# Output projection of a hybrid encoder block as seven products of halves, with its weight sums made by adding DMAs, the convolution's norm moved into the attention loop, and normalised rows transposed once

## The chip, the cores and the metric

The kernel runs on one core of one Trainium2 chip. The metric is device time in microseconds (us) of one execution, as the median over several runs; lower is better. A core has five engines with in-order queues that meet only through semaphores: TensorE (PE, matrix multiplies and transposes, writes to PSUM), VectorE (DVE), ScalarE (ACT), GpSimd (POOL) and SyncE (SP, which here only issues DMAs). PSUM holds accumulators, SBUF everything else.

## What is computed

```python
h = rms_norm(x, norm1_g); z = h @ w_in
a, gate, q, k, v = split(z)
conv = silu(layer_norm(depthwise_conv(a * sigmoid(gate), 31 taps) + bias))     # 512 channels
attn = neighbourhood_attention(rms_norm(q), rms_norm(k), v, rpb)               # 8 heads of 64
x = x + concat(conv, attn) @ w_out                                             # 1024 x 1024 x 1024
h = rms_norm(x, norm2_g)
x = x + (silu(h @ w_gate) * (h @ w_up)) @ w_down                               # 2816 hidden
```

There are 1024 tokens (16 grid rows of 64) and 1024 channels, all in float32. Accuracy is kept by splitting each matmul operand into a high part `hi`, which a cast rounds to float32r, and a low part `lo`, which is the source less `hi`: `mac` (L110) issues three matmuls for each product of two 128-deep blocks (hi by hi, hi by lo, lo by hi). `split` (L103) makes the pair: a cast on ACT (L104), then a subtraction on DVE or POOL (L108).

## The kernel before

The order of the work is written out by hand: no scheduler moves anything. A list `woven` holds small pieces of side work; after each three matmuls PE's program pops one piece (`weave`, L119), so that the side work is issued between matmuls in a fixed place. Tiles come from rings: `G` (22 buffers of 128x1024), `R` (3 raw weight chunks), `H` (6 of 128x4096), and in PSUM `mm` (4 banks), `tp` (2 banks) and `cv` (two banks as one). A new tile waits until the one that held its buffer has been read for the last time.

**Stages, in order.** (1) The input projection for keys, convolution, queries and values, with the convolution's 31 taps beside it on DVE (L319) and, for some taps, on ACT and POOL (L344, L345). Each `step` (L411) closes one 128x512 block. (2) The attention loop (L789 to L814): 32 iterations `i`, each of them one pair of heads for one tile of 128 queries. An iteration issues the score matmuls of `i` (L615), the POOL scaling of the softmax of `i-1` (L637), the transposes of `i-2` (L646) with their evacuations on ACT and DVE (L651), bias, minimum and exponential of `i` (L628 on DVE, L630 on ACT), and the value matmuls of `i-3` (L662). The evacuations of a finished tile (`evac_hi`, `evac_lo`) and two weight chunks of `w_out`, cut in four parts each (`take_parts`, L156), go between them. (3) The output projection: eight token tiles, two halves of 512 output columns, eight 128-deep blocks, three matmuls each (`proj`, L720): 384 matmuls of 128x512 into banks `pj` (first half) and `pk` (second half). Between them, the convolution is transposed to rows (`conv_T`, L728), normalised (`conv_stats`, `conv_scale`), transposed back (L761), given its activation and split (`conv_silu`). `resid` (L775) adds each half to `x`, `norm2` and `norm2_out` (L867) make the second norm. (4) The gate and up projections as seven products of halves (Winograd's form of Strassen's scheme) for each of 22 pairs of column blocks: `products` lists them, `product` (L1013) issues 12 matmuls, `evac` (L1024) combines the seven results. The left operands `A11`, `A12`, `S1` to `S4` and `A22` are the normalised rows, their halves and sums of halves, each transposed on its own by PE (`t2_one`, L994, and `s_T`, L963) and then split. The weight sums come from `t_sums` (L893, DVE), the weight splits from `prep`. (5) The down projection, again as seven products, with sums kept in DRAM.

The weights of `w_out` come as eight chunks of 128x1024 (`want`, `issue`, `take`), in order, three in flight, each load issued by SP when the buffer of an earlier chunk comes free.

Of the kernel before, what the change touches and what calls it, by code (L numbers as in the profile page):

```python
# [7 lines left out]
F32R = mybir.dt.float32r  # L8
AF = mybir.ActivationFunctionType
# [21 lines left out]
def layout(v):  # L31
# [4 lines left out]
    gu = np.stack([f["w_gate"], f["w_up"]]).reshape(2, KB, P, FB, P).transpose(3, 0, 2, 1, 4)  # L36
    wd = f["w_down"].reshape(FB, P, D)
# [14 lines left out]
        "wo": f["w_out"],  # L52
# [15 lines left out]
def build(ctx, tc, a):  # L68
# [24 lines left out]

    def mm(name):
        return ps.tile([P, 512], F32, tag="mm", bufs=4, name=name)
# [35 lines left out]
    def want(src, name, dst, sub=(pool,)):  # L131
        chunks.append((src, name, dst, sub))

    def issue():
        if pos[0] < len(chunks):
            src, name, _, _ = chunks[pos[0]]
# [4 lines left out]
            nc.sync.dma_start(d, src)  # L141
            pos[0] += 1

    def take(n=1, ahead=True):
        for _ in range(n):
            i = pos[1]
            while pos[0] <= i:
                issue()
            _, _, dst, sub = chunks[i]
# [37 lines left out]
    wo, woq = {}, {}  # L187

    def wo_dst(d, k0):
        def dst():  # L190
            if (d, k0 // 4) not in woq:
                woq[d, k0 // 4] = H(f"wo{d}{k0}", F32R)
            q = woq[d, k0 // 4]
            o = k0 % 4 * 1024
            hl = (q[:, o:o + 1024], q[:, o + 1024:o + 2048])
            for j in range(2):
                wo[d, k0 + j] = [w[:, j * 512:(j + 1) * 512] for w in hl]
            return hl
        return dst

    for d in range(2):
        for k0 in (4, 6, 0, 2):
            want(a["wo"][k0 * P:(k0 + 2) * P, d * 512:(d + 1) * 512].rearrange("(k p) m -> p k m", p=P),
                 f"wo{d}{k0}", wo_dst(d, k0), (pool,) * 4 if d == 0 and k0 < 4 else (pool,))
# [204 lines left out]
    pend = []  # L409

    def step(post=None, n_taps=4):  # L411
        todo = pend[:]
# [251 lines left out]

    def evac_hi(s_):
        rh, cb = order[s_]
        if rh == 0:
            at[cb] = [G(f"at{cb}{w}", F32R).rearrange("p (c t q) -> p c t q", c=4, t=2) for w in range(2)]
        act.copy(at[cb][0][:, :, rh], os_[s_])

    def evac_lo(s_, cs=slice(0, 4)):
        rh, cb = order[s_]
        hi, lo = [w[:, cs, rh] for w in at[cb]]
        dve.tensor_tensor(lo, os_[s_][:, cs], hi.bitcast(F32), OP.subtract)
# [38 lines left out]
    cm, x2, xn = [], {}, {}  # L713

    def lhs(k, t):
        if k < 4:
            return [w[:, k, t * P:(t + 1) * P] for w in cm]
        return [w[:, k - 4, t // 4, :] for w in at[t % 4]]

    def proj(t, d, acc, ks):  # L720
        for k in ks:
            mac(acc, lhs(k, t), wo[d, k], k == 4, k == 3)
            weave()

    def conv_T(t):
        y = cv(f"y{t}")[:, :512] if t in (0, 3) else tp(f"y{t}")
# [4 lines left out]
    cs = {}  # L731

    def conv_stats(t, y):
        st6, mv, sd = SM(f"bs{t}", 6), SM(f"bm{t}", 2), SM(f"bd{t}", 1)
        dve.bn_stats(st6, y)
        dve.bn_aggr(mv, st6)
        act.activation(sd, mv[:, 1:2], AF.Sqrt, bias=eps)
        cs[t] = y, mv, sd
        if 1 <= t <= 4:
            conv_scale(t - 1)  # L740
        if t >= 4:
            conv_scale(t)

    def conv_scale(t):
        y, mv, sd = cs.pop(t)
        r = SM(f"br{t}", 1)
        dve.reciprocal(r, sd)
        if t % 2 == 0:
            xx = G(f"xh{t}")
            xh.extend([xx[:, :512], xx[:, 512:]])  # L750
        if t >= 6:
            dve.tensor_scalar(xh[t], y, mv[:, 0:1], r, op0=OP.subtract, op1=OP.mult)
        else:
            nb = SM(f"bb{t}", 1)
            dve.scalar_tensor_tensor(nb, mv[:, 0:1], -1.0, r, OP.mult, OP.mult)
            act.activation(xh[t], y, AF.Identity, bias=nb, scale=r)

    def conv_silu(h, c):
        y = tp(f"z{h}{c}")
# [3 lines left out]
        hi, lo = [w[:, c, h * 512:(h + 1) * 512].rearrange("p (b i j) -> p i b j", b=4, j=16) for w in cm]  # L763
        split(hi, lo, y.rearrange("p (i b j) -> p i b j", b=4, j=16), (dve,))
# [9 lines left out]
    def resid(t, d, acc):  # L774
        dve.tensor_tensor(x2[t][:, d * 512:(d + 1) * 512], acc, x2[t][:, d * 512:(d + 1) * 512], OP.add)  # L775

    acc0, xh = [], []

    def attn_half(t):
        acc0.append(mm(f"pj{t}"))  # L780
        proj(t, 0, acc0[t], range(4, 8))

    def fill(*ks):
        if not acc0:
            act.activation(warm, eps, AF.Sqrt)
            acc0.append(mm("pj0"))
        proj(0, 0, acc0[0], ks)

    for i in range(2, 32 + 2):  # L789
# [4 lines left out]
        if i in (6, 12):  # L794
            load_window(i // 6)
        if i in (14, 22):
            take_parts(jobs)
        if i < 32:
            ss = score_mm(i)
        if i >= 32:  # L800
            fill(*((4, 5) if i == 32 else (6,)))
# [6 lines left out]
        flip_out(i - 2, 0)  # L808
        if i > 2:
# [3 lines left out]
            elif i > 6 and i % 4 in (0, 3):  # L813
                evac_lo((i + 1) // 4 - 2, slice(0, 2) if i % 4 == 3 else slice(2, 4))  # L814
        if jobs and i % 4 < 2:
            jobs.pop(0)()
    fill(7)

    cm += [H(f"cm{w}", F32R).rearrange("p (k s) -> p k s", s=S) for w in range(2)]
    conv_stats(0, conv_T(0))  # L820
    woven.extend([lambda: (weigh(31), evac_hi(7), evac_lo(7)), lambda: conv_stats(1, conv_T(1)), lambda: None])
    for t in range(2, 8):
        woven.extend([lambda t=t: conv_stats(t, conv_T(t)), lambda: None])
    take()
    attn_half(1)
    take()
    attn_half(2)
    attn_half(3)
    cc = cv("pj45")
    acc0 += [cc[:, :512], cc[:, 512:]]  # L830
    proj(4, 0, acc0[4], range(4, 8))
    act.activation(warm, eps, AF.Silu)
    conv_silu(0, 0)
    proj(5, 0, acc0[5], range(4, 8))
    for t in range(6):
        load_x2(t)
    later = [(0, c) for c in range(1, 4)] + [(1, c) for c in range(4)]
    woven.extend(lambda q=q: conv_silu(*q) for q in later)
    for ts in (range(4), (4, 5)):
        for k in range(4):  # L840
            for t in ts:
                mac(acc0[t], lhs(k, t), wo[0, k], False, k == 3)
                if t % 2:
                    weave()
        for t in ts:
            resid(t, 0, acc0[t])
    for t in range(6, 8):
        load_x2(t)
        acc0.append(mm(f"pj{t}"))
        proj(t, 0, acc0[t], (4, 5, 6, 7, 0, 1, 2, 3))  # L850
        take(2)
        resid(t, 0, acc0[t])
# [15 lines left out]

# [379 lines left out]
```

## Time and profile before

| | us |
|---|---|
| median of 3 runs | 1063.63 (1063.32 to 1063.68) |
| the profiled execution | 1064.03 |
| its span, first to last instruction | 1062.2 |
| PE, DVE, ACT, POOL busy | 1045.4, 699.8, 443.7, 397.3 |
| attention loop, output projection, first products | about 241 to 311, 312 to 416, 416 on |

The profile is of one execution. Busy times of PE are modelled, since matmuls overlap in a pipeline: a row's duration is longer than the distance to the next row, and that distance is the price of a matmul when PE has no other wait. In a list of groups, "x32" is the number of instructions, then their total time and the mean in nanoseconds of one, then the engine's idle time just before them with what ended it. In a timeline the bracket at the end gives the idle time before the row and its releaser. In the table by stretches, "(x90)" is the number of instructions.

### The profile page before, as it was taken

To read this page: it belongs to the slowest core of one execution; us is meant where nothing else is said; L and a number is where in the kernel's file an instruction comes from. 1 tells how busy PE (TensorE), PEld (TensorE's weight loads), DVE (VectorE), ACT (ScalarE), POOL (GpSimd) and SP (SyncE) were. 2 spreads that over 40 slices of the span, in tenths; PEclk is the share of its full clock that TensorE was granted. 3 is DMA by queue.
4 is the path that set the end of the run, shared out by engine and by line. 5 is a ranking of instruction groups with operands and counts; after the bars stand their busy time and mean duration, and the time that the engine had idled before them with its cause. 6 is when DMAs were issued, how large, how long until landed. Compare 5 with 4: busy or idle time off the path is not lost.

```text
span 1062.2 us, 13969 instructions
## 1 busy us (share of the span) xinstructions
PE 1045.4 (98%) x5068; PEld 847.3 (80%) x5068; DVE 699.8 (66%) x1072; ACT 443.7 (42%) x874; POOL 397.3 (37%) x308
## 2 busy tenths in 40 slices
PE   7999999999999999999999999999999999999997
PEld 5788888776667888788888888888888888888886
DVE  6768998966765247666565564564655567858883
ACT  6456346626776334532323223332233344433441
POOL 0126568823542301444554544545454200002310
PEclk9999999999999999999999999999999999999999
DMA  9416681245504412032322222232132597634641
GB/s 333 164 47 225 217 257 36 75 161 154 165 34 161 136 80 99 21 129 77 136 91 104 109 99 95 104 129 100 70 131 78 194 322 276 209 99 132 205 127 43
DMA packets 68244, 144.05 MB, mean 136 GB/s; under 512 B 12496, under 2 KB 21200, under 8 KB 67536
## 3 DMA queue, kind: packets, MB, share of 16 engines
q1 hardware_dynamic: 66336, 139.95, 38.3%
q10 hardware_dynamic: 1840, 3.22, 0.9%
q8 instruction: 40, 0.66, 0.3%
q14 instruction: 28, 0.23, 0.1%
HBM read 103.99 MB, written 44.76 MB: 140 GB/s over the span
## 4 chain that ended last, share of the span: by engine, by line
PE 94%; DMA 2%; DVE 1%; ACT 1%; POOL 1%; issue 0%; SPq 0%; POOLq 0%; ACTq 0%
PE B L112 6%; PE B L114 6%; PE B L113 6%; PE A L112 4%; PE D L112 4%; PE D L114 4%; PE A L114 4%; PE D L113 4%; PE A L113 4%; PE z L113 3%; PE z L112 3%; PE z L114 3%; PE gl L114 3%; PE gl L112 3%; PE gl L113 3%; PE o L662 2%
## 5 line engine op out<-in xcount | busy, mean ns | idle before, releaser
L319 DVE SCALAR_TENSOR_TENSOR cv<-u,par,cv 128x1009 f32<-128x1009 f32 (+14 forms) x85 | 108.5, 1276 | 1.9
L345 POOL TENSOR_TENSOR pa<-pa,pr 128x1022 f32<-128x1022 f32 (+10 forms) x31 | 74.2, 2392 | 35.5 <-ACT pr L344 26.5
L104 ACT CAST op<-sr 128x512 fp32r<-128x512 f32 x77 | 47.7, 619 | 52.1 <-PE B2d L114 26.3
L108 DVE TENSOR_TENSOR op<-sr,op 128x512 fp32r<-128x512 f32 x77 | 57.1, 742 | 16.1 <-ACT op L104 16.0
L1037 DVE TENSOR_TENSOR g<-B,g 128x512 f32<-128x512 f32 x22 | 15.2, 691 | 79.0 <-PE B L114 79.0
L1209 POOL TENSOR_TENSOR ou<-ou,resm 128x512 f32<-128x512 f32 x8 | 12.2, 1530 | 144.0 <-DMA resm<-xd 142.1
L1046 ACT ACTIVATE D<-D 128x512 f32<-128x512 f32 x22 | 12.8, 582 | 113.1 <-DVE D L1045 113.1
L1032 DVE TENSOR_TENSOR u<-B,g 128x512 f32<-128x512 f32 x22 | 15.2, 691 | 62.1 <-PE B L114 62.1
L104 ACT CAST op<-wd 128x512 fp32r<-128x512 f32 x66 | 40.9, 620 | 30.7 <-DVE wd L1124 18.4
L637 POOL TENSOR_SCALAR e<-e,rs 128x288 f32<-128x288 f32 (+1 forms) x64 | 34.1, 545 | 50.2 <-DVE rs L635 42.9
L108 DVE TENSOR_TENSOR op<-wd,op 128x512 fp32r<-128x512 f32 x66 | 50.4, 764 | 1.8
L893 DVE TENSOR_TENSOR ts<-gu,ts 128x512 f32<-128x512 f32 x44 | 51.0, 1159 | 0.8
L1035 ACT ACTIVATE A<-A 128x512 f32<-128x512 f32 x20 | 11.6, 582 | 76.3 <-PE A L114 76.3
L630 ACT ACTIVATE e<-e,mx 128x288 f32<-128x288 f32 (+1 forms) x64 | 36.2, 569 | 2.0 <-DVE mx L628 2.0
L628 DVE CUSTOM_DVE_ANT_0 e<-s,tab 128x288 f32<-128x288 f32 (+1 forms) x64 | 30.1, 505 | 8.1 <-PE s L615 8.0
L344 ACT ACTIVATE pr<-u,par 128x1022 f32<-128x1022 f32 (+10 forms) x31 | 34.2, 1135 | 1.2 <-ACT vs L405 1.2
L893 DVE TENSOR_TENSOR ts<-gu 128x512 f32<-128x512 f32 x22 | 34.1, 1551 | 0.0
L646 PEld LDWEIGHTS p<-ident,e 128*96 128x96 f32 (+1 forms) x192 | 20.1, 133 | 15.2 <-issue 10.5
L944 POOL TENSOR_TENSOR xn<-xn,xn 128x512 f32<-128x512 f32 x4 | 6.9, 1732 | 57.3 <-DVE sn L944 57.3
L646 PE MATMUL p<-ident,e 128*96 128x128 f32 (+1 forms) x192 | 27.6, 280 | 0.7 <-DVE pT L651 0.6
L662 PE MATMUL o<-pT,vw 96*64 96x128 f32 (+1 forms) x384 | 28.0, 281 | 0.0
L615 PE MATMUL s<-kT,qT 64*128 64x288 f32 (+1 forms) x128 | 26.7, 495 | 0.0
(1039 smaller groups left out, 3449.6 us busy)
## 6 DMA issues: line engine op xcount, KB each, us to landing
gu<-in_gu SPq DMA_DIRECT2D x44, 512.0 KB
sr<-sd SPq DMA_DIRECT2D x77, 256.0 KB
sd<-sd SPq DMA_DIRECT2D x22, 512.0 KB
wd<-in_wd SPq DMA_DIRECT2D x44, 256.0 KB
sd<-g SPq DMA_DIRECT2D x33, 256.0 KB
x<-in_x SPq DMA_DIRECT2D x16, 512.0 KB
xd<-x SPq DMA_DIRECT2D x8, 512.0 KB
resm<-xd SPq DMA_DIRECT2D x16, 256.0 KB
```

The source lines that it names most:

```text
L104: act.copy(hi, src)
L108: eng.tensor_tensor(*[w[..., sl] for w in (lo, src, hi.bitcast(F32))], OP.subtract)
L112: pe.matmul(acc, lh, rh, start=start, stop=False, skip_group_check=True)
L113: pe.matmul(acc, lh, rl, start=False, stop=False, skip_group_check=True)
L114: pe.matmul(acc, ll, rh, start=False, stop=stop, skip_group_check=True)
L319: dve.scalar_tensor_tensor(acc[:, o], uc[:, i], dwk[:, c, t:t + 1], acc[:, o], OP.mult, OP.add)
L344: act.activation(pr[:, o], uc[:, i], AF.Copy, scale=dwk[:, c, t:t + 1])
L345: pool.tensor_tensor(pa[:, o], pa[:, o], pr[:, o], OP.add)
L630: act.activation(e[:, hh], e[:, hh], AF.Exp, bias=mx, scale=-1.0, accum_out=rs[:, hh:hh + 1])
L646: pe.transpose(pt[:m, g * P:(g + 1) * P], es[i][:, hh, g * m:(g + 1) * m], ident)
L662: pe.matmul(os_[s_][hh * HD:(hh + 1) * HD, hp], vw[cb, rh + g][:, c:c + HD], pTs[i][:, g, hh], start=g == 0, stop=g == 2)
L893: dve.tensor_tensor(o, l, r, OP.subtract)
```

## The change

1. **Seven products.** `w_out` and its left operand are cut in halves both ways; the product is made as seven products of 512x512x512 (`n1` to `n7`, `group`), 4 x 4 x 3 = 48 matmuls each, 336 in all. Left operands: `a11` (attention, lower grid rows), `A12`, `A22` (convolution, the two halves of the tokens) and `Q1` to `Q4`, sums of quarters that stay in feature-major form: DVE makes them from the PSUM results of attention (`evac_lo`) and of the convolution (`conv_diff`), and ACT and POOL split them (`q_split`). `n7` accumulates on `n1`'s banks, `n5` on `n6`'s. `read` adds the banks to `x2` on DVE: `put`, 40 of them, where `resid` had 16.
2. **Weight sums by DMA.** The right operands `P1`, `P3`, `P4` are a load by SP and then a second DMA issued by POOL with `accum_op=OP.add` into the same raw chunk in SBUF (`add`, at iterations 15, 25 and 30 of the attention loop and three times in the projection). `P2` is summed in DRAM: a copy issued by ACT and two adding DMAs by POOL at fixed steps of the input projection (`at_step`), for `w_out` and for the first four column blocks of the gate and up weights (`g4`). Signs are turned so that all sums are additions. `w_out` takes 14 chunks of 128x1024 instead of 8, four of them in the attention loop. For the first four column blocks the `t_sums` on DVE go; their raw chunks for `P1`, `P3`, `P4` get six adding DMAs from POOL, beside `prep`.
3. **Convolution norm in attention.** In iterations 3, 5, ... 17, `conv_norm` transposes one token tile of the convolution (the former L728), takes its statistics on DVE and copies it to SBUF on ACT. In iterations 19 to 21 DVE makes the inverse root of all eight variances by Newton steps (`rsqrt`, 13 small instructions), in place of a square root on ACT for each tile. In iterations 22 to 29 DVE applies mean and root, one tile each (`conv_scale`, a `tensor_scalar` from SBUF to SBUF).
4. **Rows turned once.** `turn` transposes each normalised token tile once (16 groups of four transposes for eight tiles) into `xT`; the sums of halves are made from that (`s_sum`), and `s_split` splits them without PE. Before there were 8 groups at L994 and 20 at L963. The first 28 products (four column blocks) come in another order, `prep` splits their weights on POOL alone, and a table `plan` sets the side work of the first 14.

Cut to its core:

```diff
-    for d in range(2):
-        for k0 in (4, 6, 0, 2):
-            want(a["wo"][...], f"wo{d}{k0}", wo_dst(d, k0), (pool,) * 4 if d == 0 and k0 < 4 else (pool,))
+    for n in ("B11", "P3", "P4", "P2", "P1", "B21", "B22"):
+        for j in range(2):
+            src, *more = [block("w4", m)[64 * j:64 * j + 64].rearrange(...) for m in SUM.get(n, (n,))]
+            want(src, f"{n}{j}", wq_dst(n, j), more=more[0] if more else None)
...
+    def add():
+        if pending:
+            pool.dma_start(*pending.pop(0), accum_op=OP.add)
...
+    def conv_norm(t):
+        y = conv_T(t)
+        st6 = SM(f"bs{t}", 6)
         dve.bn_stats(st6, y)
+        dve.bn_aggr(mvs[:, t], st6)
+        act.copy(xh[t], y)
...
+    def conv_scale(t, eng):
+        eng.tensor_scalar(xh[t], xh[t], mvs[:, t, 0:1], rc[:, t:t + 1], op0=OP.subtract, op1=OP.mult)
...
     for i in range(2, 32 + 2):
-        if i in (14, 22):
+        if i in (17, 21, 25, 29):
             take_parts(jobs)
+        if i in (15, 25, 30):
+            add()
...
+        if i % 2 and i < 19:
+            conv_norm(i // 2 - 1)
+        if i == 19:
+            root = rsqrt(rc, mvs[:, :, 1], "rc")
+        if 19 <= i < 22:
+            next(root)
+        if 22 <= i < 30:
+            conv_scale(i - 22, dve)
...
+    group("n1", CB[1:])
+    group("n7")
+    group("n4")
+    group("n6")
+    group("n5")
+    group("n2")
+    group("n3")
...
+    def turn(t, j):
+        pt = (tp, mm)[j](f"t2{t}{j}")
+        for i in range(4):
+            kb = 4 * j + i
+            pe.transpose(pt[:, i * P:(i + 1) * P], xn[t][:, kb * P:(kb + 1) * P], ident)
```

More of the change, by code (lines that the diff above doesn't have):

```diff
@@ L141, in issue @@
             nc.sync.dma_start(d, src)
+            if more is not None:
+                pending.append((d, more))
             pos[0] += 1
@@ L813, in build @@
             elif i > 6 and i % 4 in (0, 3):
-                evac_lo((i + 1) // 4 - 2, slice(0, 2) if i % 4 == 3 else slice(2, 4))
-        if jobs and i % 4 < 2:
+                evac_lo((i + 1) // 4 - 2, (0,) if i % 4 == 3 else (1,))
+        if jobs:
             jobs.pop(0)()
[L817 to L852, printed above, removed]
+    fill(3)
     sd2 = {}
@@ new lines, in N, with U, SS, SP @@
+    def N(t):
+        return lambda: norm2_out(t)
+    def U(t, j):
+        return lambda: turn(t, j)
+    def SS(t, *ns, eng=dve):
+        return lambda: s_sum(t, ns, eng)
+    def SP(n, t, eng=dve):
+        return lambda: s_split(n, t, eng)
+    lo2 = lambda: rest.pop(0)()
+    def group(p, cbs=CB):
+        for cb in cbs:
+            more = p in ("n7", "n5")
+            if not more:
+                pb[cb] = mm(f"{p}{cb}")
+            proj(p, cb, pb[cb], start=not more)
+            read(p, cb)
@@ L1009, in build @@
+    assert not pending
     sd = dr.tile([QF, P, 7 * 512], F32, name="sd")
```

471 lines of the change are left out of this document (291 added, 180 removed).

## The prediction

> **What bounds the kernel now.** I read the page first: how busy PE is, and whether the chain that ended last runs through it.
>
> ```profile
> span 1062.2 us, 13969 instructions
> PE 1045.4 (98%) x5068; PEld 847.3 (80%) x5068; DVE 699.8 (66%) x1072; ACT 443.7 (42%) x874; POOL 397.3 (37%) x308
> PEclk9999999999999999999999999999999999999999
> PE 94%; DMA 2%; DVE 1%; ACT 1%; POOL 1%; issue 0%; SPq 0%; POOLq 0%; ACTq 0%
> ```
>
> PE is never slowed by its clock, and 94% of the chain is PE's own work. Whatever leaves PE's queue comes off the time, unless something else becomes late; so the question has two halves, how much PE work goes and what waits appear. For the price of PE work I take the timeline of PE between the attention loop and the steady products.
>
> ```profile
> 311.54 0.50 PE L112 MATMUL pj<-wo,at 128*128 128x512 f32 x1
> ...
> 324.26 0.60 PE L728 MATMUL y<-ident,u 128*128 128x128 f32 x4
> ...
> 326.08 0.60 PE L728 MATMUL y<-ident,u 128*128 128x128 f32 x4
> ...
> 416.05 0.39 PE L112 MATMUL A<-h,t0m 128*128 128x512 f32 x1
> ...
> 462.37 0.39 PE L112 MATMUL B<-S,t1m 128*128 128x512 f32 x1
> ...
> 465.09 0.39 PE L112 MATMUL A<-h,t2m 128*128 128x512 f32 x1
> ```
>
> From 462.37 to 465.09 lie 12 matmuls: 2.72 us, so 0.2267 us for one. From 324.26 to 326.08 lie one group of four transposes and six matmuls: 1.82 less 6 x 0.2267 = 1.36 leaves 0.46 us for a group. Now the groups, to see that these two prices explain the whole stretch from 311.54 (first matmul of the output projection) to 465.09 (third column block).
>
> ```profile
> L112 PE MATMUL pj<-wo,at 128*128 128x512 f32 x32 | 13.7, 429 | 0.0
> L113 PE MATMUL pk<-wo,cm 128*128 128x512 f32 x32 | 12.5, 389 | 0.0
> L728 PE MATMUL y<-ident,u 128*128 128x128 f32 x32 | 4.8, 274 | 0.0
> L761 PE MATMUL z<-ident,xh 128*128 128x128 f32 x32 | 4.8, 272 | 0.0
> L994 PE MATMUL t<-ident,xn 128*128 128x128 f32 x32 | 5.0, 274 | 0.6 <-DVE xn L867 0.6
> L963 PE MATMUL sq<-ident,xn 128*128 128x128 f32 x24 | 3.6, 272 | 0.0
> L963 PE MATMUL sp<-ident,sn 128*128 128x128 f32 x16 | 2.1, 272 | 0.0
> ```
>
> The first two are the first and the last of twelve groups of 32: 384 matmuls. L963 has four groups, 24 + 24 + 16 + 16 = 80 transposes, the first and the last shown. The stretch holds 384 + 14 x 12 = 552 matmuls, 125.1 us; 8 + 8 + 8 + 20 = 44 groups of transposes, 20.2 us; and some 4 us of attention's last transposes and value matmuls. That is 149.3 of 153.6 us: all idling of PE here comes to about 4.3 us.
>
> **The change part by part.** *Seven products:* 336 matmuls for 384, 48 x 0.2267 = 10.9 us less. The new left operands are sums in feature-major form and bring no transposes. *Rows turned once:* 64 transposes where there were 32 + 80, so 16 groups for 28, 12 x 0.46 = 5.5 us less. *Convolution norm:* its 8 groups (3.7 us) move into attention. They cost the same there, since PE is the bound there too; net nothing, if nothing else is late. Together PE loses 16.4 us.
>
> Next, attention, where DVE and ACT get more to do. Two stretches of four iterations each, the first with 288 keys, the second with 384, and within the second the gaps of DVE and ACT.
>
> ```profile
> 263.18:272.31 9.13, 9.13 (x90) 6.18 (x90) 6.80 (x27) 6.55 (x22) 3.94 (x8) 1.00 0.63 184
> 291.95:301.78 9.83, 9.83 (x90) 6.30 (x90) 7.55 (x27) 7.78 (x24) 5.98 (x10) 1.00 0.12 41
> ```
>
> ```profile
> 295.40 0.17 DVE L635 RECIPROCAL rs<-rs 128x2 f32<-128x2 f32 x1 [0.31 <-ACT e L630]
> 297.86 0.17 DVE L635 RECIPROCAL rs<-rs 128x2 f32<-128x2 f32 x1 [0.64 <-ACT e L630]
> ```
>
> ```profile
> 296.15 0.48 ACT L651 COPY pT<-p 128x384 f32<-128x384 f32 x1 [0.48 <-PE p L646]
> 301.06 0.48 ACT L651 COPY pT<-p 128x384 f32<-128x384 f32 x1 [0.30 <-PE p L646]
> ```
>
> An iteration takes 2.28 us early and 2.46 us late, all of it PE. DVE has 0.64 us to spare in a late iteration, 0.31 where half of `evac_lo` falls. ACT has 0.48 with a weight part in it and 0.30 with an `evac_hi`; the two are issued together in a few iterations only. The prices of what is added:
>
> ```profile
> L735 DVE BATCH_NORM_STATS2 bs<-y 128x6 f32<-128x512 f32 x8 | 5.6, 695 | 2.4 <-PE y L728 2.4
> L736 DVE BATCH_NORM_AGGREGATE bm<-bs 128x2 f32<-128x6 f32 x8 | 1.5, 182 | 0.3
> L752 DVE TENSOR_SCALAR xh<-y,bm,br 128x512 f32<-128x512 f32 x2 | 1.6, 810 | 0.1
> L383 DVE TENSOR_SCALAR r<-r,r x16: 230/231/1526, 24.6 to 203.5; 128x8 f32<-128x8 f32 x16
> L674 DVE TENSOR_TENSOR at<-o,at 128x256 fp32r<-128x256 f32 x14 | 5.8, 412 | 0.0
> L637 POOL TENSOR_SCALAR e<-e,rs 128x384 f32<-128x384 f32 x32 | 18.3, 586 | 7.7 <-DVE rs L635 7.7
> ```
>
> Iterations 3 to 17: statistics add 0.88 us to DVE in every other iteration, which PE's own new group lengthens by 0.46; DVE has more room early (6.80 of 9.13), so I cost this at nothing. ACT's copy of a 128x512 tile lies under the same cover. If that cover were gone, the overrun is 0.88 - 0.46 = 0.4 us in each of 8, 3 us. Iterations 19 to 21: 13 small instructions at about 0.2 us (between 0.18 at L736 and 0.23 at L383) are 2.6 us, and the doubled half evacuations of iterations 19 and 20 two times 0.82 (L674 twice), against 3 x 0.64 to spare: 2.3 us over. Iterations 22 to 29: `conv_scale` is bounded by 0.23 (L383) and 0.81 (L752, which reads PSUM); I take 0.6 because the tile is L752's, but lies in SBUF, and the doubled evacuations come at 27 and 28: 4.8 + 1.6 against 8 x 0.64 = 5.1, 1.3 over. The sum is 3.6 us. The pipeline forgives about 1 us (a softmax is scaled an iteration before PE turns it); waits for POOL (next paragraph) give about as much back. I take **+3.5 us**, between nothing (shorter scalars, hidden) and 11.
>
> L383's three durations show a mechanism. Its usual 0.23 us becomes 1.5 twice; both times it ends as a POOL instruction ends:
>
> ```profile
> 172.21 1.52 DVE L383 TENSOR_SCALAR r<-r,r 128x8 f32<-128x8 f32 x1
> ```
>
> ```profile
> 171.30 2.40 POOL L108 TENSOR_TENSOR w21l<-w21r,w21h 128x1024 fp32r<-128x1024 f32 x1
> ```
>
> 172.21 + 1.52 = 173.73, and 171.30 + 2.40 = 173.70: this kind of DVE instruction, SBUF to SBUF, stood still until POOL was done. `conv_scale` and five of the 13 small instructions are of this kind, 13 in all, and in the late iterations POOL is at work 1.17 us on softmax scaling (2 x 0.586) and 0.73 on a weight part. The Trainium skill states this as a rule (SBUF — State Buffer, section "Who interferes with whom"): whichever of DVE and GpSimd issues first holds the shared pair of ports for its whole instruction, the other blocks fully, and `tensor_scalar` is among the operations that can need the pair. The trace agrees, with 1.52 us for 0.23. Worked fully, it is the first rival.
>
> *The projection stretch.* The adds to the residual grow from 16 to 40, and sums of quarters are new:
>
> ```profile
> L775 DVE TENSOR_TENSOR x<-pk,x 128x512 f32<-128x512 f32 x8 | 5.5, 687 | 6.0 <-PE pk L114 6.0
> L108 DVE TENSOR_TENSOR cm<-z,cm 128x512 fp32r<-128x512 f32 x8 | 5.5, 692 | 11.8 <-ACT cm L104 11.8
> 311.54:465.09 153.55, 152.40 (x778) 123.64 (x777) 85.27 (x143) 69.81 (x121) 39.50 (x32) 1.00 0.26 93
> ```
>
> DVE gains 24 x 0.69 = 17 us of adds and 12 x 0.69 = 8 of `conv_diff`, and loses the statistics; it was busy 85 of 154 us, so it fits on average. It doesn't fit in `n1`: eight adds 5.5, the last evacuation 4 x 0.41, two convolution parts at 0.69 and four sums at 0.69 are 11.3 us for about 8.6 us of PE. What is queued behind are the reads that free `n1`'s banks for `n7`, but each bank is needed again only about four 2.7 us quarters of a product later, and `n7` gives the room back. POOL makes `q_split`'s and `take`'s low parts, 2.4 us each (the row of 171.30), at most four in a product of 10.9 us. At each of six borders PE can wait for the last low part: bounds 0 and 6 x 2.4 = 14 us. Then `turn` waits on `norm2_out`, as L994 did for 0.6 us. I take 4.5 us of idling, near the 4.3 of the old stretch, where the same engines did the same kinds of work: **+0.2 us**.
>
> *DMAs.* No row shows a DMA issued by POOL or one that adds. The nearest:
>
> ```profile
> 2.17 0.57 SPq L218
> 2.78 5.89 DMA wk1r<-in_qkv
> ```
>
> Issuing took SP 0.57 us, and a 512 KB chunk needed 5.89 us among other loads. An adding DMA follows its load, so the chunk is ready two such times after issue, some 12 us; the adds are issued 10 to 24 us before the split (for instance iterations 15 and 25, ten times 2.3 to 2.5 us apart), so I count nothing for landing. POOL pays about 0.6 us for an issue, between 0 and 5.9 if it has to wait for the load; a late iteration leaves it 2.46 - 1.9 = 0.56. Nothing on the path. The Trainium skill (DMA: Bandwidth & Descriptors, "Anatomy of one DMA") prices a DMA from GpSimd at about 2.0 us plus bytes over 436 GB/s, by which I estimate 3.2 us for a chunk; by that the sum would stand too. The DRAM sums run beside the input projection, far ahead of use, and the dropped `t_sums` only unload DVE.
>
> **Sum:** -10.9 - 5.5 + 3.5 + 0.2 = -12.7 us. On the profiled execution's 1064.03 (span 1062.2 and 1.8 around it) that is 1051.3; the median of the runs, 1063.63, lies 0.4 below, so 1050.9, said as **1051.0**.
>
> **The rivals.** *DVE becomes the bound in late attention.* If each of the 13 `tensor_scalar`s first sits out one POOL scaling of 0.586, 7.6 us come on top, and DVE, not PE, sets iterations 19 to 29: about 1058.5. L383's rows speak for it; that 14 of its 16 took 0.23 speaks against. Chance 0.18. *More hides than I think:* DVE's overrun vanishes and the new stretch idles little, -16.4 and part of the old 4.3: about 1044. Against it: POOL's tight borders. Chance 0.08. *The seven products save nothing:* PE waits about 2 us at each of the six borders, 12 us: about 1063. Chance 0.05. *Slower: POOL stands at the adding DMAs.* At iterations 15, 25 and 30 POOL must see the chunk landed before it can issue; behind the wait stands the softmax scaling, for which PE's next transposes wait. With a wait of 5.9 us, less 0.56 spare and 1 of slack, 4.3 us are lost three times, 13 us; if the three adds in the projection hold up the low parts by as much less 2.4 (3 x 1.9), it is about 1070. It decides from about 4.2 us each. For it: nothing of POOL's DMA price is seen. Against: the loads are issued iterations ahead. Chance 0.10.
>
> **How the numbers follow.** The forecast (1046 to 1055) keeps 0.59. Runs here agree within 0.04%, and a difference of 0.2%, 2 us, can be told from none. Faster by more than that: 0.59 + 0.18 + 0.08, and a little of the third rival, 0.86; within it 0.04; slower 0.10. The range of 1045 to 1061 takes the forecast, the first rival and the upper edge of the hidden case; 0.2 is left out.
>
> **What would show it.** Right: PE's instructions fall by 48 matmuls and 48 transposes, with the 0.2267 us kept; first `n1` matmul to fifth column block shorter by about 20 us (16.4 and the moved 3.7), attention longer by 7. DVE's gaps in iterations 19 to 29 gone. Wrong: `conv_scale` well over 0.6 us with its ends on POOL's, gaps of PE before the first matmul of `n7`, `n6` or `n5` over 2 us each, or the softmax scaling late behind a POOL DMA.

## The result, and the profile after

The changed kernel takes 1070.79 us (median of 6 runs, 1067.34 to 1073.84), the kernel before 1063.66 beside it (1063.32 to 1064.14): a ratio of 1.0064, 95% interval 1.0044 to 1.0084. It is slower, where 1051.0 and "faster" were forecast, and its runs spread over 6.5 us where those of before lie within 0.8. The profiled execution took 1071.48 us, 7.45 more than before's.

First the page, the lines that answer to those of before:

```profile
span 1069.8 us, 13910 instructions
PE 1035.9 (97%) x4972; PEld 836.4 (78%) x4972; DVE 733.1 (69%) x1097; ACT 463.7 (43%) x911; POOL 454.5 (42%) x346
PEclk9999989999999999999999999999999999999999
PE 73%; DMA 6%; SPq 5%; POOL 5%; DVE 5%; issue 3%; ACT 2%; POOLq 0%; ACTq 0%; DVEq 0%
```

PE lost its 96 instructions, 48 matmuls and 48 transposes, as forecast. Yet its share of the chain fell from 94% to 73%: the rest went to transfers, to SP's queue, to POOL and to DVE. In one slice the granted clock is below full.

Three marks on the timeline of PE cut the span: the first score matmul of attention, the first `n1` (before: `pj`) matmul, the first matmul of the fifth column block.

| stretch (us) | before | after | forecast | measured |
|---|---|---|---|---|
| up to the first score matmul | 227.56 | 232.91 | 0 | +5.4 |
| attention, to the first output product | 83.98 | 91.36 | +7.2 | +7.4 |
| output products to the fifth block | 191.63 | 185.89 | -19.9 | -5.7 |
| the rest of the span | 559.0 | 559.6 | 0 | +0.6 |

(The forecast's terms are placed here: -16.4 - 3.7 + 0.2 in the third stretch, 3.7 + 3.5 in the second.) Attention came out as forecast. Two stretches went wrong, by 5.4 and by 14.2 us. The windows of the third stretch in the two kernels, before first; after the length come busy time and count of PE, PEld, DVE, ACT and POOL, then granted clock, DMA share and GB/s:

```profile
311.54:503.17 191.63, 190.47 (x946) 155.17 (x945) 108.76 (x170) 79.71 (x139) 59.37 (x46) 1.00 0.27 97
```

```profile
324.27:510.16 185.89, 173.02 (x818) 138.89 (x817) 126.70 (x157) 91.49 (x156) 104.21 (x71) 0.99 0.54 158
```

Before, PE was idle 191.63 - 190.47 = 1.16 us by this count; after, 12.87. DMA's share doubled and POOL's work nearly did.

What PE waited for in that stretch stands on its timeline; the bracket holds the idle time and its releaser. (Where the text below speaks of a gap of PE, it is the distance between two starts less the 0.2267 us of a matmul, about 0.15 us more than the bracket.)

```profile
351.66 0.50 PE L122 MATMUL n<-wP,Q 128*128 128x512 f32 x1 [1.27 <-DVE x L864]
357.66 0.47 PE L122 MATMUL n<-wP,A 128*128 128x512 f32 x1 [2.99 <-DVE x L864]
371.10 0.50 PE L123 MATMUL n<-wP,Q 128*128 128x512 f32 x1 [1.04 <-POOL wP L118]
403.07 0.66 PE L1064 MATMUL t<-ident,xn 128*128 128x128 f32 x4 [0.98 <-DVE h L1073]
457.63 0.47 PE L122 MATMUL B<-S,t0m 128*128 128x512 f32 x1 [2.65 <-ACT S L114]
```

The engine named is the last one, so I look at what that engine had waited for. DVE, at the adds to the residual, and POOL, at one of its additions:

```profile
356.23 1.29 DVE L864 TENSOR_TENSOR x<-x,n 128x512 f32<-128x512 f32 x2 [2.83 <-DMA x<-in_x]
```

```profile
365.42 0.87 POOL L148 DMA_DIRECT2D P10r<-in_w  x1 [11.59 <-DMA P10r<-in_w]
```

DVE waited for residual tiles, POOL stood 11.59 us at an addition because its chunk was not yet loaded. SP's rows show why both came late, and the chain of waits how long one of the tiles took:

```profile
343.23 0.32 SPq L157 DMA_DIRECT2D P21r<-w4P  x1
343.65 2.71 SPq L860 DMA_DIRECT2D x<-in_x  x4
351.33 0.34 SPq L157 DMA_DIRECT2D P10r<-in_w  x1
```

```profile
343.65 12.49 DMA x<-in_x
```

Four residual tiles go out behind one chunk and ahead of the next, and the chunk P10 lands only about 14 us after its own issue.

The 5.4 us ahead of attention have another place, SP's queue around 101 us, before and then after:

```profile
102.39 8.05 SPq L481 DMA_DIRECT2D t<-in_rpb  x12
110.54 0.84 SPq L141 DMA_DIRECT2D w00r<-in_qkv  x1
```

```profile
100.94 13.46 SPq L513 DMA_DIRECT2D t<-in_rpb  x12
115.77 0.34 SPq L157 DMA_DIRECT2D w00r<-in_qkv  x1
```

```profile
101.41 1.23 POOL L217 DMA_DIRECT2D w4P<-in_w  x1
102.30 1.42 POOL L217 DMA_DIRECT2D g4P<-in_g  x1
```

While POOL's two additions into DRAM run, the same twelve bias-table stores take 13.46 us instead of 8.05. Each later load of weights in SP's order is 5 to 6.5 us later, and PE meets that at the value product:

```profile
152.70 0.79 PE L123 MATMUL z<-w03l,hT 128*128 128x512 f32 x1 [3.45 <-POOL pa L368]
```

```profile
149.84 2.81 POOL L118 TENSOR_TENSOR w03l<-w03r,w03h 128x1024 fp32r<-128x1024 f32 x1
```

The bracket names the instruction that POOL starts next; what PE needs is the low part w03l, which POOL ends at 152.65 because the chunk came late.

My theory after this: the loss comes from transfers, namely the DRAM additions, the residual loads placed among the weight chunks, and POOL waiting at additions for late chunks; the terms for PE and for attention stand. The rival: DVE and POOL have too much to do, in attention and at the borders of the seven products, and the transfers only look late. A third suspect were the first column blocks, where DVE and POOL work side by side on rows in SBUF.

### The profile page after: what moved, and what is told of

It is laid out like the page before. It is cut to its first block, busy times and chain, and to the rows that moved or that the text cites. A ratio compares the mean times of both kernels' runs of the same rounds, so it can differ in the third digit from the quotient of the medians.

```text
span 1069.8 us, 13910 instructions
## 1 busy us (share of the span) xinstructions
PE 1035.9 (97%) x4972; PEld 836.4 (78%) x4972; DVE 733.1 (69%) x1097; ACT 463.7 (43%) x911; POOL 454.5 (42%) x346
## 4 chain that ended last, share of the span: by engine, by line
PE 73%; DMA 6%; SPq 5%; POOL 5%; DVE 5%; issue 3%; ACT 2%; POOLq 0%; ACTq 0%; DVEq 0%
PE B L124 5%; PE B L122 5%; PE B L123 5%; PE D L122 3%; PE D L124 3%; PE D L123 3%; PE A L122 3%; PE A L124 3%; PE A L123 3%; PE z L123 3%; PE z L122 3%; PE z L124 3%; SPq L513 3%; PE p L678 2%; PE o L694 2%
## 5 line engine op out<-in xcount | busy, mean ns | idle before, releaser
L114 ACT CAST op<-sr 128x512 fp32r<-128x512 f32 x77 | 47.7, 619 | 53.5 <-PE B2d L124 21.7
L118 DVE TENSOR_TENSOR op<-sr,op 128x512 fp32r<-128x512 f32 x77 | 58.3, 757 | 16.4 <-ACT op L114 16.3
L983 DVE TENSOR_TENSOR ts<-ts,gu 128x512 f32<-128x512 f32 x36 | 43.3, 1203 | 0.6
L864 DVE TENSOR_TENSOR x<-x,n 128x512 f32<-128x512 f32 x40 | 26.2, 683 | 22.4 <-PE n L124 12.3
L983 DVE TENSOR_TENSOR ts<-gu 128x512 f32<-128x512 f32 x18 | 30.0, 1667 | 0.0
```

What stands on the lines that cost most here:

```text
L114: act.copy(hi, src)
L118: eng.tensor_tensor(*[w[..., sl] for w in (lo, src, hi.bitcast(F32))], OP.subtract)
L983: dve.tensor_tensor(lr(tsum[i, 1])[n - 3] if o is None else o, l, r, OP.add)
```

## The experiments

All ran beside the kernel before, whose median was 1063.2 to 1063.7 us each time.

**The DRAM additions.**

```diff
-    at_step = {5: ("w4", "B12"), 6: ("g4", "B12"), 14: ("w4", "B11"), 15: ("g4", "B11"), 32: ("w4", "B22"),
-               34: ("g4", "B22")}
+    at_step = {5: ("w4", "B12"), 6: ("g4", "B12")}
```

> Left out: the four additions into DRAM, so the block sum there holds only its first block. Theory (transfers): the changed kernel's 5.36 us later start of attention (232.99 us after the start instead of 227.63) comes from the additions of steps 14 and 15, which slow the bias-table stores and with them SP's weight loads. The first score matmul falls back to 227.6 +/- 0.5, PE's 3.45-us gap before the value product and the halved clock after it go, and the time is about 5.4 us below the changed kernel's 1070.8: 1065.4. Rival (engines): the later start comes from work on DVE and POOL; then it stays near 233 and the time at 1070 to 1071.

Measured: 1066.42 us, 1.0028 of before (1.0016 to 1.0040), 4.4 us under the changed kernel; first score matmul at 227.01. The bias-table stores are quick again:

```profile
101.52 9.02 SPq L512 DMA_DIRECT2D t<-in_rpb  x12
110.64 0.40 SPq L157 DMA_DIRECT2D w00r<-in_qkv  x1
```

The stalls in the value product are gone: the theory holds for this stretch, by all of it (5.9 us in the profile). Some came back later. The waits for residual tiles grew from 5.0 to 7.0 us, with two of 3.3 us, so the output products took 189.05 us instead of 185.89.

**The residual tiles.** `x` lies a second time in the inputs, in the order of the tiles (a permutation, no arithmetic):

```diff
+        "xr": f["x"].reshape(2, 8, 4, 16, D).transpose(0, 2, 1, 3, 4).reshape(8, P, D),
...
-        nc.sync.dma_start(x2[t], rows(a["x"], t))
+        nc.sync.dma_start(x2[t], a["xr"][t])
```

> Only the residual loads change: each row tile is read from one 512-KB block of a relaid copy of x, instead of as 8 separate groups of 16 rows. Theory (transfers): the tiles arrive late at the reads of n7, and PE loses 0.37 + 1.44 + 3.15 = 5.0 us there to DVE waiting for them; a load that uses more of the transfer engines at a time halves their 12 us, PE's gaps at these reads fall to 1.5 us or less in all, and the time falls by 3 to 5 us, to 1066 to 1068. Rival (engines): DVE has too much to do in n1 and n7 and the loads only look late; the gaps stay, 1070 to 1071.

Measured: 1062.26 us, 0.9985 of before (0.9975 to 0.9994): 8.5 us less, twice what I expected. Two windows around the second batch of tiles, the changed kernel and this one (the columns as above, DMA share and GB/s last):

```profile
344.00:351.00 7.00, 6.17 (x28) 4.44 (x26) 1.97 (x4) 2.98 (x4) 2.09 (x1) 1.00 0.65 200
```

```profile
346.00:352.00 6.00, 6.00 (x30) 4.94 (x29) 4.07 (x7) 2.37 (x4) 2.40 (x1) 1.00 0.93 363
```

The same kind of stretch moves 363 GB/s instead of 200. The Trainium skill (DMA: Bandwidth & Descriptors, section "Why a DMA increments its semaphore by 16 and not by 1") says that a transfer is spread over the largest number of engines up to 16 that divides the slowest dimension of both its patterns; the old pattern is 8 groups of 16 rows, which makes 8 engines, the new one 128 rows, which makes 16. The traces agree: the semaphore of an old tile is raised eight times when its data lands, that of a relaid tile sixteen times; between 346.8 and 351.3 us of the changed kernel 8.1 packets of 4 KB are under way in the mean, here between 349.6 and 353.0 us 15.9, and a packet takes 0.16 us in both. (The second window also holds the load of the next chunk.) PE's gaps at the reads are gone, and so are those that the expectation left alone: POOL's wait at the addition fell from 11.59 to

```profile
356.23 0.87 POOL L149 DMA_DIRECT2D P10r<-in_w  x1 [1.36 <-DMA P10r<-in_w]
```

because the chunk's load stands behind the tiles on the same queue: in the changed kernel eight of the chunk's sixteen landing signals came 4.2 us after its issue, the other eight 11.6 to 13.5 us after; here all sixteen came within 6.8 us. With it went the borders after it (1.20, 0.41, 1.15 and 0.56 us): the output products took 176.56 us, 9.3 less.

**The chunk additions.** `add()` drops the pending addition without issuing it:

```diff
-            pool.dma_start(*pending.pop(0), accum_op=OP.add)
+            pending.pop(0)
```

> Left out: the six additions into the weight chunks of the output projection (P3, P4, P1 then hold their first block only). Theory (transfers): POOL's waits of 11.59 and 1.36 us for the chunk before it can issue an addition go, its low parts are no longer bunched, and PE's gaps at the borders after n7 (1.20 and 0.41 us) and one part of those before them go: 2 to 4 us less, 1067 to 1069. Rival (engines): the borders of the seven products wait for q_split and conv_silu whatever the additions do; the gaps stay and the time is 1070 to 1071.

Measured: 1064.77 us, 1.0011 of before (0.9998 to 1.0025): 6.0 less, more than expected. PE's gaps at the reads fell here too, from 5.0 us to 0.7, with one of 1.1 behind them where PE waited for DVE's split of an operand; the transfers of the additions had stood beside those of the tiles. The two experiments overlap: each removes most of the same 8 us. But the second keeps all additions, so in the output products the additions cost next to nothing once the tiles are quick. It is the slow tiles with the additions among them that cost there, not POOL's issuing.

In attention it is otherwise. Without the additions the loop took 89.74 us instead of 91.36, 1.6 less; three of its iterations are shorter by 0.57, 0.40 and 0.54 us, at and behind the additions of iterations 25 and 30. The changed kernel shows why: the softmax scaling stands behind the issue, and PE's transposes wait for it.

```profile
307.22 0.88 POOL L148 DMA_DIRECT2D P31r<-in_w  x1
307.86 1.42 POOL L669 TENSOR_SCALAR e<-e,rs 128x384 f32<-128x384 f32 x2
308.78 1.10 PE L678 MATMUL p<-ident,e 128*128 128x128 f32 x6 [0.28 <-POOL e L669]
```

**The norm in attention.** `rsqrt` and `conv_scale` are not called.

> Left out: the reciprocal root and the eight scalings of the convolution rows inside attention (13 + 8 DVE instructions). Theory (transfers): only the attention loop gets shorter, by the 3.5 us that iterations 19 to 29 lost: first score matmul to first n1 matmul 87.8 us instead of 91.28, the stretch behind it unchanged at 186 +/- 1, time 1067.3. Rival (engines): the overload of DVE reaches on into n1 and n7; then the stretch behind attention shrinks too, by some 5 us, and the time is 1062 or less.

Measured: 1069.11 us, 1.0055 of before (1.0042 to 1.0068): 1.7 less. Attention took 89.00 us instead of 91.36, the stretch behind it 184.44 instead of 185.89; neither the 87.8 of the theory nor the 5 us more of the rival. The norm is worth 2.4 of the 3.7 us that attention lost beyond the moved transposes.

**Both mends.** With the relaid tiles, and the additions of steps 14 and 15 behind the bias tables:

```diff
-    at_step = {..., 14: ("w4", "B11"), 15: ("g4", "B11"), 32: ("w4", "B22"),
+    at_step = {..., 26: ("w4", "B11"), 28: ("g4", "B11"), 32: ("w4", "B22"),
```

> The relaid residual tiles of the second experiment, and the two additions into DRAM of steps 14 and 15 at steps 26 and 28, behind the bias tables; nothing is left out. Theory (transfers): the two costs lie in different stretches and add up. The first score matmul is back at 227 to 228 us (234.46 in the second experiment), the wait for w02 and w03 in the value product goes, and the time is about 5 us under the second experiment's 1062.3: 1057 to 1058, under the kernel before. Rival: the additions then slow the last value weights or the first tables and value windows as they slowed the first; the gaps appear before the w2 products or the first scores, attention starts after 231, and the time stays above 1060.

Measured: 1056.36 us, 0.9932 of before (0.9921 to 0.9944). The first score matmul is at 226.44, the output products take 176.57 as with the tiles alone: the two costs add up, and the change is now faster than before. PE's share of the chain is back at 88%:

```profile
PE 88%; DVE 4%; POOL 3%; ACT 2%; DMA 2%; issue 1%; SPq 0%; POOLq 0%; ACTq 0%; DVEq 0%
```

What is left of the 14 us lies in the first column blocks: two gaps, 2.82 us before the product of t0m in m5 and 1.76 before t3m. At the first, DVE's queue in this kernel:

```profile
428.81 7.65 DVE L1035 TENSOR_TENSOR xT<-xT,xT 128x512 f32<-128x512 f32 x4
436.37 4.65 DVE L119 TENSOR_TENSOR S<-xT,S 128x512 fp32r<-128x512 f32 x4
440.95 0.68 DVE L1184 TENSOR_TENSOR u<-B,g 128x512 f32<-128x512 f32 x1
```

The third row reads the first sum out of the bank that the waiting product needs. PE had finished that sum at about 436; the read starts at 440.95, behind four row sums that take 7.65 us, 1.9 in the mean, where one alone takes 0.69, while POOL makes low parts and row sums of its own:

```profile
430.00 2.98 POOL L1031 TENSOR_TENSOR s<-xT,sn 128x256 f32<-128x256 f32 x4
435.86 4.61 POOL L1031 TENSOR_TENSOR s<-xT,sn 128x256 f32<-128x256 f32 x4
440.44 1.73 POOL L119 TENSOR_TENSOR t0m<-gum,t0m 128x512 fp32r<-128x512 f32 x1
```

One by one the four sums took 4.73, 0.68, 0.68 and 1.78 us. The first ends at 433.54, 0.56 us after the last of POOL's first four row sums; the middle two fall where POOL issues a DMA; the fourth ends 0.55 us after a low part of POOL. At the second gap, before t3m, PE waits for POOL's low part, which stands behind an addition at which POOL had waited 5.42 us for the chunk. The other experiments, each on top of both mends, went to this place and to attention.

**POOL's row sums made by DVE** (`eng=pool` taken out of the plan's entries 5 and 6).

> As the run with both mends, and the fourth row sums of the first column blocks are made by DVE where POOL made them. Theory (shared port): DVE and POOL stand in each other's way there; four sums on DVE took 7.64 us instead of 2.76 while POOL made its own, and the first product sums were read 2.65 us late for PE, with a halved clock behind. With POOL's sums gone the four take 5 us or less, PE's gap before the product t0m of m5 falls from 2.8 to under 1 us, and the time is 2 to 4 us below the run with both mends: 1053.5 to 1055.5. Rival (work): DVE is simply full there; with 3 us more on it the gap stays at 2.8 us or grows, and the time is the same or 1 to 3 us longer.

Measured: 1057.07 us, 0.9933 of before (0.9921 to 0.9944): no gain. Both theories were half right.

```profile
429.75 3.79 DVE L1035 TENSOR_TENSOR xT<-xT,xT 128x512 f32<-128x512 f32 x4
433.47 6.12 DVE L1031 TENSOR_TENSOR s<-xT,sn 128x256 f32<-128x256 f32 x8
439.51 4.63 DVE L119 TENSOR_TENSOR S<-xT,S 128x512 fp32r<-128x512 f32 x4
444.07 0.68 DVE L1184 TENSOR_TENSOR u<-B,g 128x512 f32<-128x512 f32 x1
```

The four sums fell from 7.65 to 3.79 us, but the sums taken over cost DVE 6.12, and the read came later still (PE's gap: 4.99 us). The gap before t3m vanished. So I needed a run in which nobody makes them.

**POOL's row sums left out:**

```diff
             if n == 4:
-                ...
                 continue
...
-            split(sop[n][0][t], sop[n][1][t], s4[t // 2][:, t % 2], (eng,))
+            split(sop[n][0][t], sop[n][1][t], lr(xT[t + 4])[0], (eng,))
```

> As the run with both mends; left out are POOL's eight fourth row sums (S4 is then split from other rows), so neither POOL nor DVE has that work. It tells apart what moving the sums to DVE could not: whether POOL's holding of the shared port, or DVE's own load, makes PE wait in the first column blocks. Theory (shared port): the four sums on DVE take about 3.8 us instead of 7.65, as when the work was moved, and with no 6 us more behind them the first product sum is read 3 us earlier: PE's gap of 2.8 us before t0m of m5 falls under 0.7 us, the gap of 1.7 us before t3m goes too, and the time is 3 to 4.5 us under 1056.4: 1052 to 1053.5. Rival (DVE's own queue, or the chunks' additions): the gap stays at 2 us or more, and the time above 1055.

Measured: 1051.44 us, 0.9885 of before (0.9869 to 0.9902): 4.9 us less for 7.6 us of POOL's time.

```profile
429.36 3.78 DVE L1030 TENSOR_TENSOR xT<-xT,xT 128x512 f32<-128x512 f32 x4
```

```profile
318.34:490.11 171.77, 168.78 (x818) 138.57 (x817) 118.26 (x157) 90.94 (x156) 98.19 (x63) 1.00 0.59 172
```

The gap at t0m falls from 2.82 to 1.55 us, the one of 1.76 at t3m goes, and so does a stretch of 3.41 us at half the clock behind the first (1.7 us of matmuls; see the last section): together 4.7. (The gap doesn't fall under 0.7: DVE stood idle for 2.91 us ahead of the last S3 splits, since ACT's casts waited for a chunk to land, and beside POOL's low parts two of these three splits took 1.37 and 1.63 us instead of 0.68.) The stretch takes 171.77 us, 19.86 less than before, where -19.9 was forecast. The rule that the prediction weighed has a sentence for this (the Trainium skill, SBUF — State Buffer, "Who interferes with whom"): a DVE instruction with two inputs in SBUF contends with a GpSimd instruction that reads SBUF. The trace agrees, 1.91 us against 0.95 for one sum in the mean, and 4.73 against 1.97 for the first of the four. I had read the rule only for `tensor_scalar`. The run doesn't show that all 4.9 us come this way: without its row sums POOL also makes its low parts earlier, and PE had waited for one of these before t3m.

**The gate and up additions one preparation later** (`n_prep[1] + 3` for `+ 2`).

> As the run with both mends, and the six additions into the first gate and up chunks are issued one preparation later. Theory (POOL stands at an addition): POOL waited 2.4 to 5.4 us at these additions for the load of the chunk, and its low part t3m came 1.6 us late for PE. With 2.7 us more for the load, the waits fall to 0 to 2.7 us, PE's gap of 1.7 us before t3m goes, and the time is 1 to 2 us below the run with both mends. Rival: the addition itself, 6 us to its landing, then comes too late for the split of its chunk; ACT and POOL wait for the chunk instead, new gaps of 1 to 3 us appear before the products of P1, P3 or P4, and the time is the same or longer.

Measured: 1059.54 us, 0.9963 of before (0.9952 to 0.9975): 3.2 worse, as the rival said, with one gap of 6.6 us where it had expected 1 to 3. ACT's row in this kernel:

```profile
441.11 0.62 ACT L115 CAST t0m<-gum 128x512 fp32r<-128x512 f32 x1 [6.63 <-DMA gum<-in_g]
```

The cast waits 6.63 us for the addition to land; PE loses 6.6 us there. An addition must stand between the landing of its load and its own landing ahead of use, and here there is no later place.

**All scalings on ACT** (`activation` with bias and scale; one small DVE instruction makes the bias).

> As the run with both mends, and the eight scalings of the convolution rows in iterations 22 to 29 are made by ACT (one more small DVE instruction makes the bias). Theory (shared port and a full DVE): the attention loop loses 3.5 us there because DVE has 0.64 us to spare and the scalings take 0.67 to 2.33; on ACT the loop takes 88.5 to 89.5 us instead of 91.35, the time 2 to 3 us below the run with both mends. Rival (any engine is full): ACT has 0.30 to 0.48 us to spare in a late iteration, so some 0.3 us of each scaling stays on the path, 2.4 us in all; the loop takes 90.5 us or more and the time changes by less than 1 us.

Measured: 1057.63 us, 0.9944 of before (0.9932 to 0.9956). Attention took 93.54 us, 2.2 more: beyond the rival, ACT is the fuller engine there.

**Splits of S3 behind the read, and the norm spread over DVE and ACT.** Plan entries 7 and 8 go to 9 (the splits of S3), and S4's move up by one; the small instructions go to iterations 18, 21 and 22, the scalings to 23 to 30, four on each engine:

```diff
-        9: dict(s1=SP("S4", 0), s3=SP("S4", 1)),
+        9: dict(s0=SP("S3", 3), s1=SP("S3", 1), s2=SP("S3", 2), s3=SP("S4", 0)),
...
-        if 22 <= i < 30:
-            conv_scale(i - 22, dve)
+        if 23 <= i < 31:
+            conv_scale(i - 23, i % 4 in (0, 3))
```

> As the run with both mends (1056.4), and three of the four splits of S3 are made behind the first read of a product sum by DVE instead of ahead of it; nothing is left out. Theory (order in DVE's queue): PE waited 2.8 us before the product t0m of m5 because the read that frees the bank stood on DVE behind 7.65 us of row sums, slowed by POOL, and 4.65 us of S3 splits. With 3.5 us of splits behind the read, the read comes in time, PE's gap there falls under 0.7 us, the halved clock behind it goes, and the time is 2 to 4 us less: 1052.5 to 1054.5. Rival (DVE is full): the splits then come late for m7 three products on, and a gap of 2 us or more appears before the first product D; the time stays at 1056.

> As the run with both mends, and the norm of the convolution rows in attention is spread: its three groups of small instructions at iterations 18, 21 and 22 instead of 19, 20 and 21, where half evacuations are doubled, and the eight scalings at 23 to 30, four of them (where DVE has half evacuations) on ACT. Theory: the 3.5 us that attention loses are an overload of single iterations of DVE; spread over the spare time of both engines the loop takes 89 to 90 us instead of 91.34, the time 1 to 2.5 us less. Rival (any work added there is on the path, as the run with all scalings on ACT suggests): 91 us or more, the time unchanged.

> All mends together: residual tiles relaid, additions into DRAM later, S3 splits behind the first read, norm spread over two engines. If the costs lie in separate stretches, the gains add up: 1051 to 1053, within 2 us of the 1051.0 that was forecast for the change as it was. If they share DVE's time, it is no better than the better of the last two.

Measured: 1055.18 us, 0.9922 (0.9909 to 0.9934), for the first; 1056.16, 0.9928 (0.9916 to 0.9941), for the second; 1054.21, 0.9916 (0.9903 to 0.9930), for all together. None of the three can be told clearly from the run with both mends (0.9921 to 0.9944), and the last missed its 1051 to 1053: nearer to "no better than the better of the last two". In the first, the read did come in time, at 438.34. PE still lost 1.5 us at t0m to POOL's low part, which stood behind POOL's row sums, and the next read was late behind the moved splits:

```profile
441.69 0.50 PE L125 MATMUL B<-S,t0m 128*128 128x512 f32 x1 [1.35 <-POOL t0m L119]
446.93 0.76 PE L123 MATMUL B<-S,t1m 128*128 128x512 f32 x1 [2.67 <-DVE u L1182]
```

DVE was full, as the rival had it, only the gap was one product later and not at D; and POOL's own queue is on the path here. Attention took 90.74 us with the norm spread, 0.6 less (and 91.26 in the run with all). The last run, with nothing left out, has the lowest median of those that leave nothing out, 9 us under the kernel before. Of its lead of 1.5 us in the output products over the first of the three, a stretch at half the clock that its profile lacks is worth 1.7.

## Why the prediction was wrong

**PE's work: right.** 48 matmuls and 48 transposes left; in the run without POOL's row sums the stretch is shorter by 19.86 us where the terms made 19.9. That the two agree so closely is luck: by the busy count PE's work fell by 21.7 us there and its idling rose by 1.8, and that run leaves out work that the change needs.

**Attention: right in size, half right in cause.** +7.4 for 7.2. Of the 3.7 us beyond the transposes the norm's instructions are 2.4 (the run without them), and POOL's additions, which the prediction put at nothing, are 1.6 (the run without those); one lost iteration of 0.40 us goes with either. So the size came out partly by luck: 3.5 was forecast for DVE's new work alone. `conv_scale`'s median is as the estimate, 0.666 for 0.6, with one of 2.334 beside POOL, behind an addition (without the additions none took over 0.83):

```profile
L826 DVE TENSOR_SCALAR xh<-xh,par x8: 531/666/2334, 300.2 to 319.3; 128x512 f32<-128x512 f32 x8
```

The first rival, DVE blocked by POOL at all 13 instructions, didn't occur in attention but for that one; the mechanism was there, and struck in the first column blocks, through another kind of instruction.

**The step that failed first: "Nothing on the path", for the DMAs.** "The DRAM sums run beside the input projection, far ahead of use": their own use was far ahead, but the traffic of the two additions slowed the stores beside them (13.46 us for 8.05), and SP, which issues these in order ahead of the weights, was 5.4 us late. Moved, they cost nothing. And the chunks' adds were costed by their landing and by 0.6 us of POOL's time for an issue, against 0.56 to spare. An issue took 0.87 to 0.89 us, and in attention that was 1.6 us on the path. They landed 5.1 to 10.3 us after their issue, about the 5.89 taken from a load and more than the 3.2 worked out from the Trainium skill's figure (DMA: Bandwidth & Descriptors, "Anatomy of one DMA"), which the measurement overrules; what the step didn't look at is what SP issues between the chunks. The residual tiles moved into the middle of the products, need about twice the time of a plain tile, and each chunk behind them waits: 8.5 us by the second experiment. The prediction named no term for the tiles' loads at all.

**The step that failed second: +0.2 us for idling in the stretch,** taken "near the 4.3 of the old stretch, where the same engines did the same kinds of work". The measured total is 14.2 us over the forecast. Of this the transfers made 9.3, and POOL's row sums in the first column blocks 4.8 (176.57 to 171.77); that is all of it. The work there was not of the same kind: the old kernel made sums of rows on both engines too, but one at a time between other work, and none on DVE took over 0.70 us; the changed one makes them in rows of four beside each other. The place was not in the prediction at all, although the change lists the new sums: no term of the sum prices them.

**The slower rival: near in time, wrong in place.** "POOL stands at the adding DMAs", about 1070, chance 0.10. At iterations 15, 25 and 30 it never stood; the issue cost 0.87 to 0.89 us and followed other work at once; the scaling behind it was late by the issue alone:

```profile
277.46 0.89 POOL L148 DMA_DIRECT2D P30r<-in_w  x1
```

It stood 11.59 us from the end of `n7` on, through most of `n4`, and that was the effect of a late load; and up to 5.4 us at additions in the first column blocks. The time that the rival gave agrees by chance. The mark named for it, "gaps of PE before the first matmul of n7, n6 or n5 over 2 us each", was of the right sort, but none of those three had one; the largest, 3.15 us, came before the first matmul of `n4`, and 1.44 inside `n7`, both at reads that waited for residual tiles.

**What stays open.** How much of the cost of POOL's row sums comes through DVE, which they hold up, and how much through POOL's own queue, where low parts stand behind them, wasn't separated. The remaining 3 us between the best run (1054.21) and the forecast are mostly DVE and POOL on rows in the first blocks; no order that cures it without leaving work out was found.

## What to carry to other kernels

A transfer that is far ahead of its own use still delays whatever shares its queue or engines, so cost each added transfer by what is queued behind it, and look at the pattern of each one that is moved next to it. Before a stretch is taken to idle as the old one did, list which pairs of engines will newly work in SBUF at the same time: 7.6 us of work on POOL, which was busy for 60% of that stretch, cost 4.9 us on the path. A change that saves PE work and comes out slower may need only its transfers put elsewhere: two edits turned +0.6% into -0.7%.

## What the runs showed that I had not expected

PE's clock is halved after a wait. In the changed kernel, behind the stall at the value product (the columns as above, the clock third from the end):

```profile
148.00:152.00 4.00, 1.25 (x6) 0.69 (x4) 3.27 (x4) 3.45 (x4) 4.00 (x2) 0.95 0.91 253
152.00:156.00 4.00, 3.30 (x8) 2.62 (x9) 3.96 (x4) 0.93 (x3) 4.00 (x4) 0.50 0.83 244
156.00:160.00 4.00, 4.00 (x14) 3.15 (x13) 3.83 (x5) 1.23 (x1) 1.35 (x1) 0.69 0.87 204
```

The record of the clock shows 0.5 from 151.6 to 158.4 us and again from 458.8 to 462.2, that is 6.83 and 3.41 us, on a fixed grid of 3.413 us: the distances between these four changes, 6.83, 300.37 and 3.41 us, are 2, 88 and 1 times that. Matmuls are then 0.427 us apart instead of 0.227. Both times some 2.2 to 2.4 us of the 3.41 ahead were idle. The 3-us wait before 357.66, cut in two by the grid, had no such effect. A whole window at half the clock loses 1.7 us of matmuls, so the waits of 3.45 and 2.65 us cost up to 3.4 and 1.7 more, and the one of 2.99 nothing. In the two runs with the S3 splits moved, the same wait of 2.67 us was followed by such a window in one (446.75 to 450.17 us) and by none in the other. This is probably part of why the changed kernel's runs differ by 6 us: the mean clock of its runs lies between 0.993 and 0.999; no run separates it.
